# Chained block loads on GpSimd's queue, accumulating transfers by halves, and query/key pairs fetched onto both partition halves, in a gated-linear and differential attention layer

## The chip, the cores and the metric

The kernel runs on one core of a Trainium2 chip. The metric is device time in microseconds. Before the change three runs gave a median of 1126.08 us (1125.40 to 1127.34). Lower is better.

## The reference

One layer with two token mixers in parallel, for 256 tokens of width 2048, all in float32:

```python
h = rmsnorm(x, pre_norm_g)
proj = h @ w_in                      # 2048 columns in, eleven groups out
(a_q, a_k, a_v, a_g, a_lr, b_q, b_k, b_v, b_g, m_a, m_b) = split(proj)
gk  = log_sigmoid(a_lr @ gla_gk_w2 + gla_gk_b) / 16       # forget gate, rank 16
o_a = gla_chunked(a_q, a_k, a_v, gk)                      # 4 heads, 256 keys and 512 values each
lam = exp(lq1 . lk1) - exp(lq2 . lk2) + 0.2               # from diff_lambda
o_b = diff_attention(b_q, b_k, b_v, lam)                  # 16 heads: softmax(q1 k1) - lam * softmax(q2 k2)
o_a = rmsnorm(o_a, gla_norm_g) * silu(a_g);  y_a = o_a @ w_branch_a
o_b = rmsnorm(o_b, diff_norm_g) * (1 - 0.2) * silu(b_g);  y_b = o_b @ w_branch_b
out = (sigmoid(m_a) * y_a + sigmoid(m_b) * y_b) @ w_out
out = x + rmsnorm(out, post_norm_g)
```

The groups that `proj` is split into are what the kernel's keys stand for. Almost all of the time goes into products of the 256 token rows with weights that come from HBM.

## The kernel before, in words

**Weights and splits.** The weights are streamed in tiles of 128 partitions and worked on in halves of 128x1024. The products are done in the format float32r, so each half `r` is split in two: ScalarE copies it rounded to `hi` (L250), VectorE computes `lo = r - hi` (L251). TensorE then does three products for each piece, hi by the operand's hi and lo parts and lo by its hi part. `emit_half` loads and splits the next half in the list `seq`; `take` hands a half to TensorE's code after it has seen to it that the splits are AHEAD = 4 halves ahead. `hi` and `lo` have three buffers each. The scheduler fixes each engine's order of instructions before the run. GpSimd's and SyncE's queues of transfer issues are in order: an issue that waits holds all issues behind it.

**Stages.** First come the value columns `v0`, `v2`, `v3` (tasks such as the normalisation run beside). Then comes the stage that most of the change touches: six *sets*, each a 2x2 block product that is computed by seven block products rather than eight. In `phase_steps` each set runs the products in the order 1, 3, 5, 6, 2, 7, 4, each over two row blocks `t` and two halves `h`, 28 steps a set and 168 in all. A step has six matmuls. Between the steps stand 64 halves of *other* work, spread evenly: `v4`, the keys and queries of the gated attention (`k`, `q`), those of the first head group of the differential attention (`dq`, `dk`, spilled to HBM for later), and the merge gate `m00`. An other half has 12 to 16 matmuls.

**The chain of blocks.** A set's weights need sums of blocks. Four 1 MB buffers (`chain`) hold blocks a0, a1, b0, b1. `link` loads a plain block (L174, on SyncE's queue). When both halves of a block have been split for product 1 (or after an addition on VectorE, L205, for products 5 and 6), `accumulate` adds another block of HBM into the same buffer with an accumulating transfer of the whole 1 MB, issued on GpSimd's queue (L197). The blocks named c (L189) are plain loads on SyncE. A link of the next set can go when the buffer that it takes has been split for the last time.

**Banks.** Products 1, 6, 7 and 4 gather in one bank, `x`. After product 6 and again after product 7 VectorE reads that bank into `gr` (L744 after product 7), and only then may TensorE go on to add product 4. `right_done` and `left_done` put the gates on ScalarE (L700, L703, L708, L710), and `spill` (L126) writes `gr` and `gl` to HBM on GpSimd's queue; `fetch` (L131) reads back, on the same queue.

**After the sets.** `forget_gate` transposes the rank-16 columns, clears a tile and loads `w2` into four row groups (L502, L504 on GpSimd), splits it (L509, L510), and does the gate's matmuls (L519). Then follow `gla_scores`, the `ag` gates, and `diff_heads` for four groups of heads: keys and queries are computed channel by channel, scaled (L636 to L639) and spilled for each pair of heads. `diff_pair` runs as a task beside the large products: it fetches `dq` and `dk` of a pair (two transfers of 256 KB), `diff_split` makes `q2`, `kh` and `kl` (L917 to L922: six copies on ScalarE, four subtractions on VectorE, two memsets on GpSimd, each on 64 partitions), and TensorE does the scores (L952, L953), then transposes (L974), ScalarE copies them to `wt` (L976), and TensorE multiplies with the values (L982 to L984). In `q2` the hi part of a query lies on its own partition half and the lo part on the other; `kh` holds the hi part of the key on both halves, `kl` the lo part on its own half and zeros on the other. The output products end the kernel.

Of the kernel before, what the change touches and what calls it, by code (L numbers as in the profile page):

```python
# [7 lines left out]
F32R = mybir.dt.float32r  # L8
# [19 lines left out]
PRODUCTS = (1, 3, 5, 6, 2, 7, 4)  # L28
SETS = 6
LEAD = 6  # L30
EARLY = (0,)
STORED = (0, 1, 2, 3)
BIG = 18
MORE = 13
BRIDGE = 512
# [41 lines left out]
def phase_steps():  # L77

    keys = ["v4"] + [f"{name}{hf}{c}" for hf in range(2) for name in ("k", "q") for c in range(4)]
    keys += [f"{name}{g}{c}" for g in EARLY for pair in range(2) for name in ("dq", "dk") for c in (2 * pair, 2 * pair + 1)]  # L80
    keys += ["m00"]
    other = [(key, r, h) for key in keys for r in range(4 if key in ("v4", "m00") else 1) for h in range(2)]
    steps = [("set", s, prod, t, h) for s in range(SETS) for prod in PRODUCTS for t in range(2) for h in range(2)]
    mixed = []
    for i, step in enumerate(steps):
        mixed.append(step)
        mixed += other[len(other) * i // len(steps) : len(other) * (i + 1) // len(steps)]
    return mixed


# [1 line left out]
def hybrid_kernel(ctx: ExitStack, tc, xt, xn, preg, postg, w, w2, gkb, glag, lamv, diffg, ident_d, causal_d, lmask_d, out):  # L92
# [45 lines left out]
    def f32(ap):  # L138
        return ap.bitcast(F32)
# [27 lines left out]
    def weights(key, r):  # L167
        a, size = at[key][r]
        return w[a : a + P * size].rearrange("(p n) -> p n", p=P), size

    def link(s, name, t):
        count[0] += 1
        c = blocks.tile([P, 2048], F32, tag="chain", name=f"{name}_{count[0]}", bufs=4)
        sp.dma_start(c, weights(f"set{s}", {"a": 0, "b": 6}[name] + t)[0])  # L174
        chain[s, name, t] = c

    def emit_set(s, prod, t, h):
        c = slice(1024 * h, 1024 * h + 1024)
        if h == 0 and prod == 1:
            if s == 0:  # L180
                link(s, "a", t)
            link(s, "b", t)
        if h == 0 and prod == 4 and s + 1 < SETS:
            link(s + 1, "a", t)
        n = 4 * PRODUCTS.index(prod) + 2 * t + h + LEAD - 4 * PRODUCTS.index(2)
        if 0 <= n < 4:
            i, j = n // 2, n % 2
            raws[s, i, j] = u([P, 1024], "c")
            sp.dma_start(raws[s, i, j], weights(f"set{s}", 4 + i)[0][:, 1024 * j : 1024 * j + 1024])  # L189
        a, b = chain[s, "a", t], chain[s, "b", t]  # L190
        return raws[s, t, h] if prod == 2 else (b if prod in (3, 7) else a)[:, c]

    def follow_set(s, prod, t, h):
        c = slice(1024 * h, 1024 * h + 1024)

        def accumulate(name, i):
            pool.dma_start(chain[s, name, i], weights(f"set{s}", 2 + i)[0], accum_op=ALU.add)  # L197

        if prod == 1 and h == 1:
            accumulate("a", t)  # L200
        i = {(5, 1): 0, (6, 0): 1, (2, 1): 0, (7, 0): 1}.get((prod, t))
        if i is not None:
            a = chain[s, "a", i][:, c]
            second = prod in (5, 6)
            dve.tensor_tensor(out=a, in0=a, in1=chain[s, "b", i][:, c] if second else raws[s, i, h], op=ALU.add)  # L205
            if second and h == 1:
                accumulate("b", i)

    def emit_plain(j, key, r, h):
        src, size = weights(key, r)  # L210
        if h == 0:
            count[0] += 1
            raws[key, r] = wpool.tile([P, 2048], F32, tag="raw", name=f"raw_{count[0]}")
        raw = raws[key, r]
        n = size // 2
        early = key == "v0"
        if h == 0:
            if j == 0:
                load_x(0, 1)
            cuts = (0, n // 2, n, size) if j == 0 else (0, n, size) if j == 2 else (0, size)  # L220
            for a, b in zip(cuts, cuts[1:]):
# [268 lines left out]
    def forget_gate():  # L490
# [11 lines left out]
        pool.memset(w2_raw, 0.0)  # L502
        for i in range(4):
            pool.dma_start(w2_raw[32 * i : 32 * i + RANK, :], w2)  # L504
# [119 lines left out]


    gspill = [None] * (2 * SETS)
    ts, heads, m0 = {}, {}, []

    def merge_gate(banks):
# [11 lines left out]
    def others():  # L641
# [24 lines left out]
        for g in EARLY:  # L666
            for pair in range(2):
                for name in ("dq", "dk"):
                    t = t2([P, 2, S], name)
                    for c in range(2):  # L670
                        o = ps("bg")
                        for h in range(2):
                            half_channel(o, h, *take(f"{name}{g}{2 * pair + c}"))
                            if h:
                                head_part(t[:, c, :], o[:, :S], o[:, S:], name == "dk")
                                if c:
                                    heads[g, pair, name] = spill(t, name)
# [230 lines left out]

    obh, obl = [], []

    parts = {}

    def diff_split(g, pair, tq, tk):
        q2, kh, kl = parts[g, pair] = [u([P, 2, 2, S], name, F32R) for name in ("q2", "kh", "kl")]
        for m in range(2):
            own, other = slice(64 * m, 64 * m + 64), slice(64 - 64 * m, P - 64 * m)
            act.activation(q2[own, m], tq[own], AF.Copy)  # L917
            dve.tensor_tensor(out=q2[other, m], in0=tq[own], in1=f32(q2[own, m]), op=ALU.subtract)
            act.activation(kh[own, m], tk[own], AF.Copy)
            act.activation(kh[other, m], tk[own], AF.Copy)  # L920
            dve.tensor_tensor(out=kl[own, m], in0=tk[own], in1=f32(kh[own, m]), op=ALU.subtract)
            pool.memset(f32(kl[other, m]), 0.0)  # L922
        done.add(f"split{g}{pair}")
        yield

    def diff_pair(g, pair, values):
        oh, ol = obh[g], obl[g]
# [6 lines left out]
        if g in STORED:  # L934
            tq, tk = (fetch(heads[g, pair, name], name, lambda shape, name, dtype: t2(shape, name)) for name in ("dq", "dk"))
            yield
            yield from diff_split(g, pair, tq, tk)
        while f"split{g}{pair}" not in done:
            yield
        q2, kh, kl = parts[g, pair]  # L940
        vv, uu = values
        for h in (2 * pair, 2 * pair + 1):
            i2 = h % 2
# [62 lines left out]
    def diff_heads(g):  # L1006
        values = []
        if g + 2 >= SETS:
            banks = token_major(f"dv{g}", 512, x_ops, 2)
            late_u = u2 if g > 1 else u  # L1010
            vv = late_u([P, 2, 512], "dv")
            for b in range(2):
                act.activation(vv[:, b, :], banks[b], AF.Copy, scale=rstd[:, b : b + 1])
            banks = token_major(f"bg{g}", 512, x_ops, 2)
            uu = late_u([P, 2, 512], "ub")
            for b in range(2):
                gate(banks[b], b, uu[:, b, :])
            values += vv, uu
        obh.append(u2([P, 4, S], "obh", F32R))
        obl.append(u2([P, 4, S], "obl", F32R))  # L1020
        for pair in range(2):
            made = []
            for name in () if g in EARLY else ("dq", "dk"):
                t = t2([P, 2, S], name)
                for c in range(2):
                    head_part(t[:, c, :], *channel_major(f"{name}{g}{2 * pair + c}"), name == "dk")
                    pump(2)
                if g in STORED:
                    heads[g, pair, name] = spill(t, name)
                else:  # L1030
                    made.append(t)
            if made:
                tasks.insert(0, diff_split(g, pair, *made))
            tasks.append(diff_pair(g, pair, values))


# [197 lines left out]
```

## Time and profile before

| | |
|---|---|
| median of 3 runs | 1126.08 us |
| the profiled execution's own time | 1125.56 us |
| its span, first to last instruction | 1123.8 us |
| TensorE busy | 1101.0 us (98%) |
| VectorE, ScalarE, GpSimd busy | 852.1, 688.2, 105.6 us |
| mean granted TensorE clock | 0.996 |
| moved by the DMA engines | 264.06 MB |

The page gives the busy time of each engine, then the span in 40 equal slices with the busy share of each in tenths, then the DMA queues, the chain of work that ended last, the costliest groups of instructions, and the DMA issues with their median time to landing. A row of the timeline reads: start, duration, engine, line, operation, the tile written and the tiles read, shape and count, and in brackets the engine's idle time before it and what ended that.

### The profile page before, as it was taken

The page shows a single profiled execution, that of the slowest core. Times are in us where ns is not written, and L with a number is a line of the kernel's source. Part 1 is how long each engine was busy: PE and PEld are TensorE (multiplying, and loading weights), DVE is VectorE, ACT ScalarE, POOL GpSimd, SP SyncE. Part 2 cuts the span into 40 slices and gives each one's busy share as a digit, 9 for nine tenths or more (in the row PEclk, how much of TensorE's full clock was granted, in tenths as well). Part 3 has the DMA queues.
Part 4 walks back from the last instruction along what each step waited for, and adds up shares of the span by engine and source line. Part 5 has one row for each costly group of instructions (what it writes and reads, how often), then busy time and mean ns, then how long its engine had stood idle before and what let it go on. Part 6 is the DMA issues. An engine that isn't in the chain of part 4 may idle for free.

```text
span 1123.8 us, 15119 instructions
## 1 busy us (share of the span) xinstructions
PE 1101.0 (98%) x5546; PEld 941.8 (84%) x5546; DVE 852.1 (76%) x1192; ACT 688.2 (61%) x1011; POOL 105.6 (9%) x173
## 2 busy tenths in 40 slices
PE   8999999999999999999999999999999999999996
PEld 7997887888888888877888888888888888888886
DVE  7877969889798897966998667786777865656463
ACT  7855666666666676669555556676767664444450
POOL 0100010010101001020000221121202020000000
PEclk9999999999999999999999999999999999999999
DMA  8797897887979879666554946575677575556752
GB/s 315 259 413 206 237 327 195 334 214 224 288 214 360 209 247 316 160 213 251 187 183 159 372 153 225 179 249 210 206 245 251 200 278 197 188 187 215 272 187 76
DMA packets 47834, 264.06 MB, mean 235 GB/s; under 512 B 6096, under 2 KB 7632, under 8 KB 25232
## 3 DMA queue, kind: packets, MB, share of 16 engines
q1 hardware_dynamic: 31968, 196.50, 48.9%
q0 software_dynamic: 14784, 65.28, 21.0%
q10 hardware_dynamic: 1008, 1.32, 0.4%
q8 instruction: 43, 0.70, 0.3%
q14 instruction: 31, 0.25, 0.1%
HBM read 241.06 MB, written 22.02 MB: 234 GB/s over the span
## 4 chain that ended last, share of the span: by engine, by line
PE 85%; issue 5%; DMA 4%; ACT 2%; DVE 2%; POOL 0%; DVEq 0%; SPq 0%; POOLq 0%; ACTq 0%
PE mm L437 38%; PE mm L726 15%; PE bg L459 6%; PE mm L459 6%; DMA a<-in_w_dram 3%; PE bg L461 3%; PE mm L461 3%; PE bg L437 2%; PE bg L420 2%; PE mm L405 2%; PE mm L420 2%; DVE lo L251 1%; ACT hi L250 1%; PE bg L829 1%; PE bg L405 1%
## 5 line engine op out<-in xcount | busy, mean ns | idle before, releaser
L251 DVE TENSOR_TENSOR lo<-raw,hi 128x1024 fp32r<-128x1024 f32 (+3 forms) x291 | 345.3, 1188 | 153.9 <-ACT hi L250 144.7
L250 ACT ACTIVATE hi<-raw 128x1024 fp32r<-128x1024 f32 (+3 forms) x291 | 298.9, 1030 | 230.7 <-PE mm L437 140.1
L437 PE MATMUL mm<-hi,xs 128*128 128x512 f32 (+1 forms) x576 | 139.7, 384 | 0.0
L250 ACT ACTIVATE hi<-a 128x1024 fp32r<-128x1024 f32 x96 | 101.2, 1059 | 62.0 <-PE bg L459 19.8
L251 DVE TENSOR_TENSOR lo<-a,hi 128x1024 fp32r<-128x1024 f32 x96 | 116.4, 1220 | 26.2 <-ACT hi L250 24.8
L437 PEld LDWEIGHTS mm<-hi,xs 128*128 128x128 f32 x576 | 106.4, 188 | 16.4
L459 PE MATMUL mm<-xs,hi 128*128 128x512 f32 x384 | 101.3, 396 | 0.0
L459 PE MATMUL bg<-xs,hi 128*128 128x512 f32 x384 | 99.5, 390 | 0.7 <-ACT hi L250 0.7
L459 PEld LDWEIGHTS bg<-xs,hi 128*128 128x128 f32 x384 | 72.1, 188 | 15.3 <-ACT hi L250 1.1
L726 PE MATMUL mm<-hi,xs 128*128 128x512 f32 x288 | 77.9, 392 | 2.6 <-DVE gr L744 2.6
L459 PEld LDWEIGHTS mm<-xs,hi 128*128 128x128 f32 x384 | 69.2, 189 | 11.6
L437 PE MATMUL mm<-lo,xs 128*128 128x512 f32 (+1 forms) x288 | 74.5, 380 | 0.0
L251 DVE TENSOR_TENSOR lo<-b,hi 128x1024 fp32r<-128x1024 f32 x48 | 58.3, 1219 | 12.6 <-ACT hi L250 11.8
L250 ACT ACTIVATE hi<-b 128x1024 fp32r<-128x1024 f32 x48 | 50.7, 1060 | 24.1 <-PE bg L459 10.8
L726 PEld LDWEIGHTS mm<-hi,xs 128*128 128x128 f32 x288 | 53.1, 188 | 13.2 <-issue 2.3
L437 PEld LDWEIGHTS mm<-lo,xs 128*128 128x128 f32 x288 | 54.0, 188 | 9.0
L461 PEld LDWEIGHTS bg<-xs,lo 128*128 128x128 f32 x384 | 52.4, 190 | 4.1 <-DVE lo L251 0.3
L461 PEld LDWEIGHTS mm<-xs,lo 128*128 128x128 f32 x384 | 52.4, 190 | 3.8
L963 ACT ACTIVATE prob<-prob,mx,score_scale 128x128 f32<-128x128 f32 x64 | 34.3, 537 | 31.9 <-DVE mx L958 31.9
L461 PE MATMUL bg<-xs,lo 128*128 128x256 f32 x384 | 53.8, 282 | 0.0
L461 PE MATMUL mm<-xs,lo 128*128 128x256 f32 x384 | 53.5, 282 | 0.0
L437 PE MATMUL mm<-hi,oah 128*128 128x512 f32 x128 | 50.9, 397 | 0.0
(299 smaller groups left out, 2074.5 us busy)
## 6 DMA issues: line engine op xcount, KB each, us to landing
raw<-in_w_dram SPq DMA_DIRECT2D x128, 1024.0 KB, 5.1
a<-in_w_dram SPq DMA_DIRECT2D x12, 1024.0 KB, 6.9
b<-in_w_dram SPq DMA_DIRECT2D x12, 1024.0 KB, 8.0
c<-in_w_dram SPq DMA_DIRECT2D x24, 512.0 KB, 11.4
a<-in_w_dram POOLq DMA_DIRECT2D x12, 1024.0 KB, 14.1
b<-in_w_dram POOLq DMA_DIRECT2D x12, 1024.0 KB, 10.6
raw<-in_w_dram SPq DMA_DIRECT2D x14, 832.0 KB, 6.1
dq<-dq POOLq DMA_DIRECT2D x16, 256.0 KB, 3.7
```

The source lines that it names most:

```text
L250: act.activation(hi_t[:, a:b], r[:, a:b], AF.Copy)
L251: dve.tensor_tensor(out=lo_t[:, a:b], in0=r[:, a:b], in1=f32(hi_t[:, a:b]), op=ALU.subtract)
L405: i = pe.matmul(out, lhs, rhs, start=first and n == 0, stop=last and n == len(pairs) - 1)
L420: i = pe.matmul(banks[g][b][:, :n], a[part][:, P * b : P * b + P], w[:, n * g : n * g + n], start=first, stop=last)
L437: i = pe.matmul(banks[b][:, :n], a[part][:, P * b : P * b + P], w[:, n * j : n * j + n], start=first, stop=last)
L459: i = pe.matmul(o, hi[:, c], x_pair(kt), start=kt == 0, stop=kt == KT - 1)
L461: i = pe.matmul(o[:, :S], lo[:, c], x_ops(kt)[0], start=False, stop=False)
L726: i = pe.matmul(out, a[part], w[:, 512 * j : 512 * j + 512], start=first, stop=last, skip_group_check=out is x)
L829: pe.matmul(o, xk[:, P * c : P * c + P], xq.rearrange("p (b c t) -> p b c t", b=2, c=4)[:, :, c, :], start=i == 0, stop=i == 1)
L963: act.activation(prob[m][:, lo:up], prob[m][:, lo:up], AF.Exp, scale=score_scale[:, b : b + 1], bias=mx[:, i : i + 1], accum_out=z[:, i : ...
```

## The change

- **Order of the set stage.** FRONT = 4 other halves come one after each of the first four steps; the remaining 60 are spread over the 168 steps.
- **Block loads.** Set 0's a0 and a1 are linked when the first half of `v3` is emitted, its b0 and b1 at product 1, on SyncE as before. For sets 1 to 5 all four links are issued on GpSimd's queue, at earlier steps of the emission: a0 at (product 7, t = 1), a1 at (4, 0), b0 at (4, 1), b1 at (1, 0) of the set itself.
- **Accumulating transfers by halves.** Each 128x1024 half goes out behind its own split (or addition): 48 transfers of 512 KB for 24 of 1 MB.
- **Forget gate.** `w2_raw` is allocated before the set stage; its memset and four loads go ahead of `m00`, and the task loses its first step.
- **Pairs of the differential attention.** `diff_split` is gone. `twice` fetches the pair's `dq` into a raw tile and its `dk` into `kl`, each onto both partition halves: four transfers of 256 KB a pair. ScalarE then makes `q2` and `kh` with one full-width copy each, VectorE subtracts twice for `q2` on 64x512 and once for the whole `kl`. There are no memsets, and `kl` holds the lo part on both halves. `STORED` goes; all groups are spilled and fetched, as they were.

```diff
     mixed, put = [], 0
     for i, step in enumerate(steps):
         mixed.append(step)
-        mixed += other[len(other) * i // len(steps) : len(other) * (i + 1) // len(steps)]
+        due = min(i + 1, FRONT) + (len(other) - FRONT) * (i + 1) // len(steps)
+        mixed += other[put:due]
+        put = due
...
-        sp.dma_start(c, weights(f"set{s}", {"a": 0, "b": 6}[name] + t)[0])
+        (pool if s else sp).dma_start(c, weights(f"set{s}", {"a": 0, "b": 6}[name] + t)[0])
...
-        if h == 0 and prod == 1:
-            if s == 0:
-                link(s, "a", t)
-            link(s, "b", t)
-        if h == 0 and prod == 4 and s + 1 < SETS:
-            link(s + 1, "a", t)
+        if h == 0 and s + 1 < SETS and (prod, t) in ((7, 1), (4, 0)):
+            link(s + 1, "a", 1 - t)
+        if h == 0 and s + 1 < SETS and (prod, t) == (4, 1):
+            link(s + 1, "b", 0)
+        if h == 0 and prod == 1 and (s == 0 or t == 0):
+            link(s, "b", t if s == 0 else 1)
...
-            pool.dma_start(chain[s, name, i], weights(f"set{s}", 2 + i)[0], accum_op=ALU.add)
-
-        if prod == 1 and h == 1:
+            pool.dma_start(chain[s, name, i][:, c], weights(f"set{s}", 2 + i)[0][:, c], accum_op=ALU.add)
+
+        if prod == 1:
             accumulate("a", t)
...
-            if second and h == 1:
+            if second:
                 accumulate("b", i)
...
+        if key == "v3" and r == 0 and h == 0:
+            for i in range(2):
+                link(0, "a", i)
...
-        w2_raw, w2_s = u([P, 1024], "w2_raw"), u([P, 1024], "w2_s", F32R)
-        pool.memset(w2_raw, 0.0)
-        for i in range(4):
-            pool.dma_start(w2_raw[32 * i : 32 * i + RANK, :], w2)
-        yield
+        w2_s = u([P, 1024], "w2_s", F32R)
...
+        pool.memset(w2_raw, 0.0)
+        for i in range(4):
+            pool.dma_start(w2_raw[32 * i : 32 * i + RANK, :], w2)
         banks = [ps("bg"), ps("bg")]
         for q in range(KT // 2):
             half_tile(banks, 512, q, x_ops, *take("m00"))
...
-    def diff_split(g, pair, tq, tk):
...
+    def twice(t, d):
+
+        for h in range(2):
+            rows = slice(64 * h, 64 * h + 64)
+            pool.dma_start(f32(t[rows]), d.rearrange("(m p) i t -> p m i t", m=2))
...
-            tq, tk = (fetch(heads[g, pair, name], name, lambda shape, name, dtype: t2(shape, name)) for name in ("dq", "dk"))
-            yield
-            yield from diff_split(g, pair, tq, tk)
...
+        raw = u([P, 2, 2, S], "dq")
+        q2, kh, kl = (u([P, 2, 2, S], name, F32R) for name in ("q2", "kh", "kl"))
+        twice(raw, heads[g, pair, "dq"])
+        twice(kl, heads[g, pair, "dk"])
+        yield
+        act.activation(q2, raw, AF.Copy)
+        act.activation(kh, f32(kl), AF.Copy)
+        for m in range(2):
+            other = slice(64 - 64 * m, P - 64 * m)
+            dve.tensor_tensor(out=q2[other, m], in0=raw[other, m], in1=f32(q2[other, m]), op=ALU.subtract)
+        dve.tensor_tensor(out=kl, in0=f32(kl), in1=f32(kh), op=ALU.subtract)
+        yield
```

More of the change, by code (lines that the diff above doesn't have):

```diff
@@ L30 @@
 LEAD = 6
+FRONT = 4
 EARLY = (0,)
-STORED = (0, 1, 2, 3)
 BIG = 18
@@ L83, in phase_steps @@
     steps = [("set", s, prod, t, h) for s in range(SETS) for prod in PRODUCTS for t in range(2) for h in range(2)]
-    mixed = []
+    mixed, put = [], 0
     for i, step in enumerate(steps):
         mixed.append(step)
-        mixed += other[len(other) * i // len(steps) : len(other) * (i + 1) // len(steps)]
+        due = min(i + 1, FRONT) + (len(other) - FRONT) * (i + 1) // len(steps)
+        mixed += other[put:due]
+        put = due
     return mixed
@@ L626, in hybrid_kernel @@
     gspill = [None] * (2 * SETS)
+    w2_raw = u([P, 1024], "w2_raw")
     ts, heads, m0 = {}, {}, []
@@ L909, in hybrid_kernel @@
     obh, obl = [], []
-    parts = {}
-    def diff_split(g, pair, tq, tk):
[L914 to L923, printed above, removed]
-        yield
+    def twice(t, d):
+        for h in range(2):
+            rows = slice(64 * h, 64 * h + 64)
+            pool.dma_start(f32(t[rows]), d.rearrange("(m p) i t -> p m i t", m=2))
     def diff_pair(g, pair, values):
@@ L933, in diff_pair @@
             values.extend(fetch(gspill[2 * g + 4 + i], name, u) for i, name in enumerate(("dv", "ub")))
-        if g in STORED:
-            tq, tk = (fetch(heads[g, pair, name], name, lambda shape, name, dtype: t2(shape, name)) for name in ("dq", "dk"))
-            yield
-            yield from diff_split(g, pair, tq, tk)
-        while f"split{g}{pair}" not in done:
-            yield
-        q2, kh, kl = parts[g, pair]
+        raw = u([P, 2, 2, S], "dq")
[10 more added lines that the diff above has]
+        yield
         vv, uu = values
@@ L1021, in diff_heads @@
         for pair in range(2):
-            made = []
             for name in () if g in EARLY else ("dq", "dk"):
@@ L1027, in diff_heads @@
                     pump(2)
[L1028 to L1033, printed above, removed]
+                heads[g, pair, name] = spill(t, name)
             tasks.append(diff_pair(g, pair, values))
```

## The prediction

> **What bounds the kernel now.** I read the page first: busy time, the slices, and the chain that ended last.
>
> ```profile
> span 1123.8 us, 15119 instructions
> PE 1101.0 (98%) x5546; PEld 941.8 (84%) x5546; DVE 852.1 (76%) x1192; ACT 688.2 (61%) x1011; POOL 105.6 (9%) x173
> ...
> PEclk9999999999999999999999999999999999999999
> DMA  8797897887979879666554946575677575556752
> ...
> PE 85%; issue 5%; DMA 4%; ACT 2%; DVE 2%; POOL 0%; DVEq 0%; SPq 0%; POOLq 0%; ACTq 0%
> ```
>
> TensorE is the bound: busy for 1101.0 of 1123.8 us. The change gives it the same products, so it can win back only idle time (1123.8 − 1101.0 = 22.8 us, ends included) and time at a lower clock; anything that makes TensorE late costs in full. The table of windows says where that idle time lies (columns: window, length, busy time and count of PE, PEld, DVE, ACT and POOL, then granted clock, DMA share, GB/s).
>
> ```profile
> 75.00:100.00 25.00, 25.00 (x124) 22.64 (x123) 17.84 (x19) 14.95 (x18) 2.87 (x4) 1.00 1.03 329
> 100.00:125.00 25.00, 22.94 (x101) 19.64 (x100) 21.70 (x21) 16.16 (x18) 1.73 (x2) 0.93 0.68 172
> 125.00:150.00 25.00, 22.85 (x113) 19.62 (x112) 20.07 (x21) 16.69 (x21) 1.65 (x3) 1.00 0.81 286
> 175.00:200.00 25.00, 24.20 (x119) 19.98 (x119) 24.96 (x27) 15.73 (x18) 1.41 (x2) 1.00 0.68 156
> ```
>
> TensorE's timeline names the gaps ahead of the kernel's end, which the change does not touch (the last bracket: us idle, and what ended it).
>
> ```profile
> 103.23 0.50 PE L726 MATMUL mm<-hi,r1h 128*128 128x512 f32 x1 [2.00 <-ACT hi L250]
> 140.47 1.15 PE L726 MATMUL mm<-hi,xs 128*128 128x512 f32 x4 [2.15 <-DVE gr L744]
> 278.42 2.11 PE L459 MATMUL bg<-xs,hi 128*128 128x512 f32 x8 [0.71 <-ACT hi L250]
> 347.92 0.93 PE L726 MATMUL mm<-hi,xs 128*128 128x512 f32 x3 [0.40 <-DVE gr L744]
> 483.88 0.50 PE L437 MATMUL bg<-hi,xs 128*128 128x512 f32 x1 [0.69 <-ACT hi L250]
> 511.11 1.07 PE L519 MATMUL bg<-lrt,w_s 128*128 128x256 f32 x7 [1.30 <-issue]
> 695.74 0.30 PE L953 MATMUL bg<-kl,q 128*128 128x128 f32 x1 [0.72 <-DVE kl L921]
> 709.54 0.49 PE L982 MATMUL bg<-dv,wt 128*128 128x128 f32 x2 [1.46 <-ACT wt L976]
> ```
>
> These eight make 9.43 us; with 0.80 in 175 to 200 and the clock's loss in 100 to 125 that is what any part of the change can reach.
>
> **Step 1: set 0's accumulating transfers (FRONT, halves, early links).** The rows are the issue on GpSimd's queue, the same transfer in the chain, the split that needed it, and one "other" half on TensorE with the set half behind it.
>
> ```profile
> 86.01 0.88 POOL L197 DMA_DIRECT2D a<-in_w_dram  x1 [0.84 <-DVE vl L551]
> ...
> 86.01 16.01 DMA a<-in_w_dram
> ...
> 102.13 1.06 ACT L250 ACTIVATE hi<-a 128x1024 fp32r<-128x1024 f32 x1 [5.19 <-DMA a<-in_w_dram]
> ...
> 112.89 1.61 PE L437 MATMUL bg<-hi,xs 128*128 128x400 f32 x8
> 115.06 0.40 PE L726 MATMUL mm<-hi,s2h 128*128 128x512 f32 x1
> ...
> 141.91 1.07 PE L726 MATMUL mm<-hi,xs 128*128 128x512 f32 x4
> 143.27 1.07 PE L726 MATMUL mm<-hi,xs 128*128 128x512 f32 x4
> ```
>
> The transfer takes 16.01 us, ACT waits 5.19 for it, and TensorE, four halves behind, idles 2.00. Behind that gap the granted clock is 0.93 over 25 us, a loss of 0.07 × 25 = 1.75 us. The change moves this read later against the issue: the second block's first half goes out one set half earlier (143.27 − 141.91 = 1.36 us), and three more "other" halves lie in between (115.06 − 112.89 = 2.17 us each): 1.36 + 3 × 2.17 = 7.9 us, more than the 5.19 by which ACT was late, before counting that half a block should land sooner than a whole one. So the wait goes: −(2.00 + 1.75) = −3.75, call it −3.7. Bounds: −3.75 if all goes, 0 if the transfers stretch by as much. I take the full end because 7.9 exceeds 5.19.
>
> The Trainium skill, page "TensorE: Matmul & The Clock Gate", section "HAM oscillation — how this bites in real kernels", says that only TensorE gaps above about 3.4 us bring the clock down. By that rule the 2.00 gap has no clock loss to give back, and this term would be −2.0 and the sum 1.7 us smaller. The trace shows 0.93 behind a gap of 2.00 and 1.00 around the longer gap of 2.15, so length alone does not decide here; the measurement stands.
>
> **Step 2: set 1's second block.** ACT waits for an accumulated block once more:
>
> ```profile
> 172.75 2.01 ACT L250 ACTIVATE hi<-a 128x1024 fp32r<-128x1024 f32 x2 [3.53 <-DMA a<-in_w_dram]
> ```
>
> TensorE loses 0.80 in that window. Here the first half gains the 1.36 us of one set half, and half of the bytes to wait for; the lateness is 3.53. The page's medians to landing bound what the bytes are worth:
>
> ```profile
> a<-in_w_dram SPq DMA_DIRECT2D x12, 1024.0 KB, 6.9
> ...
> a<-in_w_dram POOLq DMA_DIRECT2D x12, 1024.0 KB, 14.1
> ```
>
> If a half takes half of 14.1, 7 us come off; if nothing, 1.36. I take −0.8 (bounds −0.8 and 0), since 3.53 − 1.36 = 2.17 is under a third of 7.
>
> **Step 3: the handover between product 7 and product 4.** DVE must read the bank (gr, L744) before TensorE writes on in it. FRONT leaves ten "other" halves to each set in one fixed pattern, where before it drifted.
>
> ```profile
> 139.64 0.68 DVE L744 TENSOR_TENSOR gr<-mm,p 128x512 f32<-128x512 f32 x1
> ...
> L726 PE MATMUL mm<-hi,xs 128*128 128x512 f32 x288 | 77.9, 392 | 2.6 <-DVE gr L744 2.6
> ```
>
> The group's 2.6 is 2.15 + 0.40 of the list above; with 0.71 and 0.69 (sets 2 and 5, an "other" half between, its split late) six handovers cost 3.95. In the changed program's order five of the six stand like sets 2 and 5, and after set 2 product 4 follows directly and must wait for the 0.68 us add and about 0.2 around it: 5 × 0.71 + 0.9 = 4.45, so +0.5. Bounds: none visible, as in sets 1 and 4 (−3.95), and 2.15 in all six (12.9 − 3.95 = +8.95).
>
> **Step 4: forget gate's w2 early.** The memset and four loads that stood after the merge gate (L502, L504) go ahead of it.
>
> ```profile
> 494.39 0.97 POOL L502 MEMSET w_raw<- 128x1024 f32 x1
> 497.22 1.94 POOL L504 DMA_DIRECT2D w_raw<-in_w_dram  x4
> 508.64 1.06 ACT L509 ACTIVATE w2h<-w_raw 64x1024 fp32r<-64x1024 f32 x1 [0.68 <-DMA w_raw<-in_w_dram]
> ```
>
> At 508.64 ACT waits for the load; the L519 matmuls then idle TensorE 1.30 at 511.11. With the data there for tens of us, their place in the program follows ready operands: −1.3 (bounds −1.3 and 0). On Pool the 0.97 + 1.94 now stand among set 5's block links; at worst those issue 2.9 us later, hidden while their data is needed later than that.
>
> **Step 5: diff attention.** Per pair, two fetches become four (256 KB each), ten split instructions and two memsets become five and none.
>
> ```profile
> 682.52 0.55 POOL L126 DMA_DIRECT2D dk<-dk  x1 [15.07 <-DVE dk L639]
> 683.06 0.54 POOL L131 DMA_DIRECT2D dq<-dq  x1
> ...
> 688.70 1.29 ACT L917 ACTIVATE q<-dq 64x512 fp32r<-64x512 f32 x2 [3.13 <-DMA dq<-dq]
> ...
> 694.90 0.69 DVE L921 TENSOR_TENSOR kl<-dk,kh 64x512 fp32r<-64x512 f32 x1
> ```
>
> One pair's fetch (683.06) stood behind a spill that waited 15.07 us for DVE; ACT then waited 3.13, kl came at 694.90, and TensorE lost 0.72 on kl and 1.46 on the wt behind it. In the changed order both fetches stand ahead of that spill: −2.2. A full-width kl subtraction (1.2 us, an estimate from the 0.69 of half the width) now sits in front of TensorE's scores where two of 0.69 stood; I book 0.4 for it: −1.8 (bounds −2.2, and +1.4 if the two gaps stay and one more of 1.4 joins). The other pairs show no gap; ACT falls from 6 × 0.65 to 2 × 1.06 us a pair.
>
> **Step 6: twenty block loads on GpSimd's queue.**
>
> ```profile
> 129.80 0.33 SPq L174 DMA_DIRECT2D a<-in_w_dram  x1
> 143.08 1.06 ACT L250 ACTIVATE hi<-a 128x1024 fp32r<-128x1024 f32 x1 [0.30 <-PE mm L726]
> 150.76 0.53 POOL L126 DMA_DIRECT2D gl<-gl  x1 [8.85 <-ACT gl L708]
> 151.37 0.89 POOL L197 DMA_DIRECT2D a<-in_w_dram  x1
> ```
>
> The links can't really go sooner: they wait for buffers freed by the same splits as before. On Pool each issue costs 0.89: 20 × 0.89 = 17.8 us, and 24 more accumulate issues at 0.53 to 0.89 are 13 to 21, and the 16 more fetches of step 5 (0.54) 9, beside 105.6 busy; Pool bounds nothing. What is queued behind a waiting link: the gr spill, the next accumulates, the gl spill. The a accumulates now stand ahead of gl's 8.85 wait, in part. I book 0 (bounds −0.5 and the price of rival C), covered by the spare time of a link: the one issued at 129.80 lands after some 6.9, near 136.7, and its first split starts at 143.08, so 6.4 us later.
>
> Fewer "other" halves in sets 1 to 5 (10 for 10.7) put more set halves against DVE, which is busy 24.96 of 25 in 175 to 200: +0.3, an estimate (0.7 × 5 halves, a tenth of a us each).
>
> **Sum**: −3.7 − 0.8 + 0.5 − 1.3 − 1.8 + 0.3 = −6.8, against the profiled execution's own 1125.56 (span 1123.8, 1.76 around it): 1118.8. The median shown, 1126.08, is 0.5 above it: 1119.3.
>
> **Rivals.** 0.2% is 2.25 us, about what a measurement of this kernel tells from none.
>
> B: the accumulates stay late because the DMA engines are full, not because they start late. For: 1.03 DMA share in 75 to 100, just while they run; early links add load there. Against: the same bytes as before, 7.9 us more room. Then steps 1 and 2 give nothing; steps 3 to 5 leave −2.3: 1123.8, on the bound.
>
> C, slower: links and accumulates share one queue. Before, block loads ran beside the accumulates from SP; now a 1 MB load of 7 to 14 us stands ahead of the next set's accumulates in Pool's queue. It decides once accumulates land some 3 us later: 3.53 us of lateness cost TensorE 0.80 and 5.19 cost 2.00 and a clock dip, 3.75. A slip of 5 us on both a blocks in each of the sets 1 to 5 costs 5 × 2.0 or so at the bare gap, 10 to 11: 1130; with the dip each time 5 × 3.75 = 18.8: 1138. For: DMA share of 0.68 to 1.03 in the set windows. Against: halves need half of the bytes, and links issue well ahead of the accumulates. The Trainium skill, page "DMA: Bandwidth & Descriptors", sections "Queues, rings and completion order" and "SWDGE vs HWDGE vs iDMA", supports this rival: each DMA engine takes turns between queue rows, while one ring drains in its order, and a plain load belongs on the hardware path. No run before shows a plain block load on Pool's queue.
>
> D: the new pattern makes the handover 2.15 in all six sets, as in set 0: +8.95 in place of +0.5, so 1127.8. For: 2.15 is the worst that the trace shows. Against: sets 2 and 5, with the order that five sets now have, paid 0.7.
>
> E: handovers vanish as in sets 1 and 4 too: −4.5 more, about 1114.8.
>
> **How the numbers follow.** Forecast (A) 0.50; B 0.14 (faster 0.08, same 0.06); C 0.18, slower; D 0.10 (same 0.05, slower 0.04, faster 0.01); E 0.08. Faster 0.50 + 0.08 + 0.01 + 0.08 = 0.67; same 0.06 + 0.05 = 0.11; slower 0.18 + 0.04 = 0.22. The time is A's, with 1116.5 to 1122.5 of its own. The range runs from 1114.0 (below E) to 1130.0 (C's cheaper half), which leaves out the rest of C, some 0.1, and little beside.
>
> **What would show it.** Step 1: no ACT wait of some us on an accumulated block near 100 us, clock 1.00 there. Step 2: PE 25.00 between set 1's products. Step 3: gaps of 0.7, not 2, ended by hi or gr. Step 4: no gap at the w2 matmuls. Step 5: no gap ended by kl or wt. Step 6: links on Pool landing in 7 to 14 us, no ACT wait on them. The prediction is wrong if ACT waits on a or b in sets 1 to 5, if "gr" ends gaps of 2 us, or if q2 or kl ends new ones.

## The result and the profile after

The changed kernel takes 1138.47 us (median of 4 runs, 1134.93 to 1141.18) against 1125.96 (1125.40 to 1127.34): a ratio of 1.0107 with a 95% interval of 1.0073 to 1.0142. It is slower by about 12.5 us. The profiled execution, 1141.18 us with a span of 1139.4, is the longest of the four.

The page of the changed kernel, the lines that answer to those of before:

```profile
span 1139.4 us, 15115 instructions
PE 1107.3 (97%) x5546; PEld 942.7 (83%) x5546; DVE 848.3 (74%) x1184; ACT 675.0 (59%) x979; POOL 142.0 (12%) x217
...
PEclk9999999999999999999999999989999999999998
DMA  9899797796988879676555965756858675556751
...
PE 84%; DMA 6%; issue 3%; DVE 3%; ACT 2%; POOL 1%; DVEq 0%; SPq 0%; POOLq 0%; ACTq 0%
```

TensorE is still the bound, ScalarE and VectorE have less to do, and yet idle time (1139.4 − 1107.3 = 32.1 us, 9.3 more) and time at a lower clock have both grown. TensorE is busy 6.3 us longer for the same 5546 matmuls; by the windows below the clock took 5.25 us (0.07 × 25 + 0.14 × 25), 3.5 more than before, and the other 2.8 are not accounted for here. The windows say where (columns as before; first three windows of the kernel before, then those of the changed one):

```profile
300.00:325.00 25.00, 25.00 (x127) 21.28 (x126) 22.83 (x22) 15.57 (x18) 1.71 (x2) 1.00 0.98 289
650.00:675.00 25.00, 25.00 (x145) 21.88 (x145) 17.32 (x29) 15.94 (x30) 4.82 (x8) 1.00 0.46 159
725.00:750.00 25.00, 25.00 (x130) 21.16 (x129) 21.00 (x39) 22.61 (x43) 7.00 (x12) 1.00 0.66 230
```

```profile
75.00:100.00 25.00, 25.00 (x129) 23.42 (x128) 15.57 (x18) 14.92 (x19) 4.65 (x6) 1.00 1.00 286
100.00:125.00 25.00, 25.00 (x122) 21.83 (x121) 23.94 (x24) 17.47 (x19) 4.54 (x6) 1.00 0.99 277
175.00:200.00 25.00, 25.00 (x125) 21.17 (x124) 24.99 (x25) 16.61 (x19) 3.42 (x4) 1.00 0.77 190
225.00:250.00 25.00, 23.15 (x113) 18.96 (x112) 17.30 (x18) 13.83 (x16) 2.77 (x5) 1.00 0.98 280
300.00:325.00 25.00, 22.77 (x110) 18.40 (x109) 17.53 (x16) 14.17 (x16) 2.18 (x3) 1.00 0.88 236
650.00:675.00 25.00, 22.58 (x129) 19.33 (x127) 18.46 (x29) 16.25 (x29) 9.46 (x14) 1.00 0.75 224
675.00:700.00 25.00, 24.89 (x140) 21.74 (x141) 16.56 (x30) 11.26 (x16) 1.14 (x2) 0.93 0.53 184
725.00:750.00 25.00, 19.82 (x102) 16.53 (x102) 17.27 (x41) 14.40 (x30) 6.43 (x8) 0.86 0.63 179
```

Set 0 (100 to 125) and set 1 (175 to 200) are now full, as predicted. New holes stand in sets 2 and 3 (225 to 250, 300 to 325) and, larger, in the differential attention (650 to 750), with the clock's loss behind two of them. TensorE's timeline names what ended the gaps:

```profile
143.44 0.50 PE L464 MATMUL bg<-xs,hi 128*128 128x512 f32 x1 [0.72 <-ACT hi L255]
246.96 0.50 PE L731 MATMUL mm<-hi,r1h 128*128 128x512 f32 x1 [1.79 <-ACT hi L255]
281.43 0.47 PE L731 MATMUL mm<-hi,xs 128*128 128x512 f32 x1 [0.88 <-DVE gr L749]
318.26 0.50 PE L731 MATMUL mm<-hi,r1h 128*128 128x512 f32 x1 [2.17 <-ACT hi L255]
420.25 0.50 PE L464 MATMUL bg<-xs,hi 128*128 128x512 f32 x1 [0.94 <-ACT hi L255]
506.67 0.48 PE L520 MATMUL bg<-lrt,w_s 128*128 128x256 f32 x2 [0.38 <-issue]
674.96 0.55 PE L894 MATMUL bg<-ident,ua 128*128 128x128 f32 x3 [2.42 <-DVE ua L887]
742.68 0.48 PE L975 MATMUL bg<-ident,prob 128*128 128x128 f32 x1 [4.99 <-DVE prob L971]
```

Both traces have 4866 matmuls with split weights. Counted through the timelines, the changed kernel is 2.6 us behind at the 2593rd (after the sets) and 15.5 behind at the 4105th (in the output products), and stays so. In this execution, then, 2.6 us were lost up to the end of the set stage, where the prediction had won some 5, and 12.9 in the differential attention, where it had won 1.8.

The list of waits has ScalarE's, which are new in the attention (us in total, times, longest):

```profile
ACT hi L255 <- DMA a<-in_w_dram: 15.7, 4, 5.9
...
ACT q L935 <- DMA dq<-dq: 15.2, 6, 4.3
...
ACT kh L936 <- DMA kl<-dk: 9.3, 5, 4.2
```

Before, ScalarE waited 3.13 us for dq in one place and 0.72 for dk in another; now 24.5 us for dq and dk. The largest gap, step by step in the changed kernel's timeline:

```profile
732.20 2.21 POOL L346 TENSOR_TENSOR de<-de,neg_half 128x2 f32<-128x2 f32 x1 [4.80 <-DVE de L992]
734.37 0.62 POOL L920 DMA_DIRECT2D dq<-dq  x1
...
738.60 1.06 ACT L935 ACTIVATE q<-dq 128x1024 fp32r<-128x1024 f32 x1 [3.60 <-DMA dq<-dq]
...
742.27 0.75 DVE L971 SCALAR_TENSOR_TENSOR prob<-prob,c,prob 128x128 f32<-128x128 f32 x2
```

The second half of a pair's dq stands on GpSimd's queue behind a 128x2 operation that waits for VectorE; ScalarE waits for that transfer; the exponentials of another pair are queued behind its q; prob comes at 742.27, and TensorE, whose order is fixed too, stood still for 4.99 us.

### The profile page after: what moved, and what is told of

Same layout as the page of the kernel before. It is cut to its first block, busy times and chain, and to the rows that moved or that the text cites. A ratio compares the mean times of both kernels' runs of the same rounds, so it can differ in the third digit from the quotient of the medians.

```text
span 1139.4 us, 15115 instructions
## 1 busy us (share of the span) xinstructions
PE 1107.3 (97%) x5546; PEld 942.7 (83%) x5546; DVE 848.3 (74%) x1184; ACT 675.0 (59%) x979; POOL 142.0 (12%) x217
## 4 chain that ended last, share of the span: by engine, by line
PE 84%; DMA 6%; issue 3%; DVE 3%; ACT 2%; POOL 1%; DVEq 0%; SPq 0%; POOLq 0%; ACTq 0%
PE mm L442 37%; PE mm L731 17%; PE bg L464 7%; PE mm L464 5%; PE bg L466 3%; DMA a<-in_w_dram 3%; PE bg L442 3%; PE mm L466 3%; DMA dq<-dq 2%; DVE lo L256 2%; PE bg L425 2%; PE mm L410 2%; PE mm L425 2%; ACT hi L255 1%; PE bg L834 1%
## 5 line engine op out<-in xcount | busy, mean ns | idle before, releaser
L442 PE MATMUL mm<-hi,obh 128*128 128x512 f32 x128 | 50.5, 394 | 0.0
```

The source lines that it names most:

```text
L442: i = pe.matmul(banks[b][:, :n], a[part][:, P * b : P * b + P], w[:, n * j : n * j + n], start=first, stop=last)
```

## The experiments

All times are medians; "before" is the kernel before on the same chip, measured anew in each round; intervals are of the ratio. Only the single transfer is more than 2% from before; the others are told from it, or not, by their intervals. Where two rows have different values of before, a difference of their times is one across rounds; the values of before differ by up to 1.2 us.

| kernel | us | before | ratio (95%) |
|---|---|---|---|
| step 5 alone | 1137.08 | 1125.41 | 1.0096 (1.0078 to 1.0115) |
| all but step 5 | 1127.86 | 1125.41 | 1.0020 (1.0008 to 1.0032) |
| all but step 5, links on SyncE | 1134.63 | 1125.41 | 1.0077 (1.0057 to 1.0097) |
| all but step 5, whole accumulates | 1132.46 | 1125.41 | 1.0058 (1.0037 to 1.0078) |
| pairs fetched into the large pool | 1127.56 | 1126.61 | 1.0016 (1.0006 to 1.0026) |
| whole change, splits two steps later | 1132.66 | 1126.61 | 1.0051 (1.0030 to 1.0072) |
| all but step 5, c on GpSimd | 1122.38 | 1126.61 | 0.9964 (0.9953 to 0.9975) |
| FRONT alone | 1138.87 | 1126.61 | 1.0110 (1.0092 to 1.0127) |
| FRONT alone, later pattern | 1128.03 | 1126.01 | 1.0026 (1.0015 to 1.0037) |
| all but step 5, c on GpSimd, later pattern | 1118.16 | 1126.01 | 0.9933 (0.9914 to 0.9952) |
| step 5 alone, one transfer each | 1229.51 | 1126.01 | 1.0917 (1.0893 to 1.0941) |
| before, four issues a pair | 1125.41 | 1126.01 | 0.9997 (0.9985 to 1.0009) |
| large pool, four issues of 128 KB | 1127.23 | 1125.40 | 1.0018 (1.0007 to 1.0028) |
| large pool, four issues of 256 KB | 1133.31 | 1125.40 | 1.0073 (1.0053 to 1.0093) |

### Which part costs: step 5 alone, and all but step 5

The first adds the diff's last part (`twice` and the full-width splits, for `diff_split`) to the kernel before; the second takes that part out of the changed kernel and leaves the rest.

```diff
-            yield from diff_split(g, pair, tq, tk)
+        twice(raw, heads[g, pair, "dq"])
+        twice(kl, heads[g, pair, "dk"])
+        yield
+        act.activation(q2, raw, AF.Copy)
...
```

> The kernel before with step 5 alone: pairs fetched onto both halves, split by full-width instructions. Theory 1 (the pair's splits stand in ScalarE's fixed order ahead of other work and wait for fetches that GpSimd's queue issues late): +10 to +14 us over before, with ScalarE idle 15 us or more ahead of q and kh for dq and dk, and gaps of 2 us or more on TensorE ended by ua or prob. Rival (the loss comes only in the surroundings that the other parts make; the step itself does what was predicted): -2 to 0 us.

> The changed kernel with the pairs of the differential attention as before, all other parts kept. Theory 1: what is left of the loss is that of the set stage, +2 to +4 us over before, and the gaps ended by ua and prob are gone. Rival (the loss behind the sets comes from another part, for instance the memory that early w2 holds): +10 us or more. The prediction's own steps 1 to 4 without step 5 would give -5.

Step 5 alone costs 11.7 us, all the rest 2.4; together 14.1, near the whole loss of 12.5. With step 5 alone ScalarE's waits on dq and kl are 9.0 + 13.0 us, and the gaps ended by ua and prob are back (2.30 and 4.64 us).

```profile
ACT kh L931 <- DMA kl<-dk: 13.0, 6, 4.4
...
ACT q L930 <- DMA dq<-dq: 9.0, 4, 3.7
```

Counted by matmuls as above, step 5 alone is level with before at the 2593rd (0.0 us) and 11.3 behind at the 4105th: its whole cost arises in the differential attention. Theory 1 holds as to the place; the step's cost does not need the other parts around it.

### The set stage: the queue of the links, and halves

```diff
-        (pool if s else sp).dma_start(c, weights(...)[0])
+        sp.dma_start(c, weights(...)[0])
```

```diff
-            pool.dma_start(chain[s, name, i][:, c], weights(...)[0][:, c], accum_op=ALU.add)
+            pool.dma_start(chain[s, name, i], weights(...)[0], accum_op=ALU.add)      # behind the second half
```

> As the changed kernel without step 5, but the twenty block loads go on SyncE's queue at the same steps. Theory 2 (block loads and accumulates share one queue, and b1's load holds back the accumulates of its own set; rival C of the prediction): the accumulates of a land about 4 us sooner in sets 2 and 3, the two gaps of 1.9 and 2.3 us ended by an accumulated a go, so 3 to 5 us faster than the changed kernel without step 5. Rival (the wait comes from the bytes on the DMA engines, whatever the queue): within 1 us of it.

> As the changed kernel without step 5, but each accumulating transfer is of a whole 1 MB block again, behind both halves. If halves help (prediction, steps 1 and 2): slower than the changed kernel without step 5 by 2 to 6 us, with longer waits of ScalarE for a. Rival (the half that lands last sets the wait, and it lands when the whole block would): within 1 us.

Theory 2 fell: with the links on SyncE the kernel is not faster but 6.8 us slower than with them on GpSimd. SyncE's timeline around set 1, first with links on GpSimd, then with links on SyncE, shows one thing that moved:

```profile
140.37 0.33 SPq L228 DMA_DIRECT2D raw<-in_w_dram  x1
141.22 1.18 SPq L192 DMA_DIRECT2D c<-in_w_dram  x2
```

```profile
150.06 0.33 SPq L177 DMA_DIRECT2D b<-in_w_dram  x1
150.49 1.65 SPq L192 DMA_DIRECT2D c<-in_w_dram  x3
```

A link waits for its buffer, and on SyncE's queue it holds the c loads behind it: three of them go at 150.49, just ahead of set 1's accumulates (issued from 152.60 on), where without the links the last two went at 141.22. The last half of a then lands 19.2 us after its issue (14.9 with the links on GpSimd), and ScalarE waits for accumulated blocks six times, 16.9 us in all, in place of four times and 11.5. The holding up is read from this one stretch; c on GpSimd's queue with the links on SyncE was not tried.

Without halves the kernel is 4.6 us slower, as predicted. The longer waits of ScalarE that were expected with it did not show: 7.7 us in three places with whole blocks, 11.5 in four with halves. The two profiled executions differ by only 1.6 us, so where the 4.6 us arise stays open.

### Set 3: the c loads

In the changed kernel the four c loads of set 3 (SyncE) go out with the accumulates of a (GpSimd), and the chain shows the last of these:

```profile
289.36 3.53 SPq L191 DMA_DIRECT2D c<-in_w_dram  x4
```

```profile
290.79 0.89 POOL L199 DMA_DIRECT2D a<-in_w_dram  x1 [2.86 <-DVE lo L256]
...
297.98 0.86 POOL L199 DMA_DIRECT2D a<-in_w_dram  x1 [1.18 <-DVE lo L256]
```

```profile
297.98 19.06 DMA a<-in_w_dram
```

```diff
-            sp.dma_start(raws[s, i, j], weights(f"set{s}", 4 + i)[0][...])
+            pool.dma_start(raws[s, i, j], weights(f"set{s}", 4 + i)[0][...])
```

> As the changed kernel without step 5, but the c loads go on GpSimd's queue too, so that in sets 2 and 3 they stand behind the accumulates of a. Theory 4 (in set 3 the four c loads of 512 KB, issued with the accumulates, take the DMA engines from them, and the last half of a lands after 19.9 us): the gap of 3.1 us near 318 and the clock's dip behind it go, 4 to 6 us faster than the changed kernel without step 5, near 1122 to 1124. Rival (order within GpSimd's queue holds the accumulates): no faster, and more gaps on c.

It is 5.5 us faster than all but step 5 (ratios to before of 0.9964 and 1.0020) and faster than the kernel before. The windows of sets 2 and 3 in this kernel:

```profile
225.00:250.00 25.00, 25.00 (x126) 21.29 (x126) 20.90 (x21) 15.69 (x18) 6.05 (x10) 1.00 1.04 286
300.00:325.00 25.00, 25.00 (x127) 21.28 (x126) 22.49 (x22) 15.92 (x18) 3.48 (x4) 1.00 1.01 287
```

In the same windows TensorE of all but step 5 was busy 24.93 and 22.03 us, so most of the gain lies in set 3; its gap there was 2.97 us, with the clock at 0.86 over that window. The DMA engines are no emptier than before (1.04, 1.01), but the c bytes now come behind the accumulates, in one queue, and TensorE is not held up. The last half of a lands 14.97 us after its issue, in place of 19.06 (19.87 in all but step 5), and the last c lands at 314.35, near the 314.42 of the changed kernel. The Trainium skill, "DMA: Bandwidth & Descriptors", section "Queues, rings and completion order", says that each DMA engine takes turns between queue rows and drains a ring in its order. The runs fit that: on another queue 2 MB of c shared the engines with the accumulates and the last half took 19.06 us, on the same queue it took 14.97. They do not prove it, since the order of the issues changed as well: the first c goes out at 294.89, just behind the last accumulate (294.34), where it went out at 289.36, ahead of the first. A later start of c on SyncE's own queue was not tried.

### FRONT, alone and with its other halves laid later

Only `phase_steps` is changed, first as in the change, then with 84 added to the quotient that places the 60 halves:

```diff
-        due = min(i + 1, FRONT) + (len(other) - FRONT) * (i + 1) // len(steps)
+        due = min(i + 1, FRONT) + ((len(other) - FRONT) * (i + 1) + 84) // len(steps)
```

> The kernel before with the four front halves alone (the order of the set stage), nothing else. Prediction, step 1: without halves the room is 3 x 2.17 + 1.36 - 1.36 = 6.5 us, still over the 5.19, so set 0's gap and the clock's dip go: -3.7, the handovers +0.5 to +1, so -3 us. Rival (other waits take the place): between -1 and +2 us, with accumulated blocks late in later sets, which have fewer other halves to cover them.

> The kernel before with the four front halves alone, but the other 60 halves laid 84/168 of a step pattern later, so that in sets 1 to 5 three of them, not two, stand between the split of a block for product 1 and its reading for product 5. Theory 5 (FRONT alone costs 12 us because each later set lost an other half in just that stretch, 2.2 to 2.8 us of cover for the accumulate): 6 to 14 us faster than the front halves alone, 1125 to 1132 us. Rival (the cost is that sets 1 to 5 have ten other halves, wherever these stand): within 2 us of the front halves alone, 1139.

FRONT alone missed both expectations: 12.3 us slower. Set 0's wait is gone, but the later sets wait (list of waits, before and with FRONT alone, and TensorE's timeline with FRONT alone in sets 1 and 4):

```profile
ACT hi L250 <- DMA a<-in_w_dram: 13.6, 4, 5.2
```

```profile
ACT hi L253 <- DMA a<-in_w_dram: 27.6, 7, 5.1
```

```profile
181.03 0.50 PE L729 MATMUL mm<-hi,r1h 128*128 128x512 f32 x1 [2.15 <-ACT hi L253]
...
393.25 0.50 PE L729 MATMUL mm<-hi,r1h 128*128 128x512 f32 x1 [1.64 <-ACT hi L253]
```

The order written by `phase_steps` gives the reason. In sets 1 to 5 of the kernel before, two or three other halves stand between the set's second step, which sends out a0's accumulate, and the ninth, which reads it, and two or three between the fourth and the eleventh (a1), five or six together; with FRONT there are two and two in each. Moving the pattern makes them three and three, with the same ten halves a set, and 10.8 of the 12.3 us come back (across rounds; 11.9 us of waits on a are left, in three places). Where the halves stand decides, not their number.

> The changed kernel without step 5, with the c loads on GpSimd's queue and the other halves in that later pattern. Theory 5: ScalarE's waits on an accumulated a, still 6 us in all with the c loads moved, go to near zero, 0 to 2 us faster than the c loads alone (1122.4). Rival (the window is wide enough already): the same within 1 us.

With both, the waits on an accumulated a are gone from the list, and the kernel takes 1118.16 us: 0.9933 of before, the fastest here. It gained more than was expected (4.2 us over the c loads alone, across rounds).

### Step 5: place, count, bytes, form

In the kernel before, a pair's fetch waits for a buffer of the small pool; in the changed one its target is in the large pool, and the order lets fetch and splits go earlier, among the gssq work. The first edit here changes that target alone, the second moves the changed kernel's splits two steps of the task back; TensorE's order in the attention changes with it.

```diff
-  lambda shape, name, dtype: t2(shape, name)
+  lambda shape, name, dtype: u([P, 2, 2, S], name)[:, 0]
```

```diff
         twice(kl, heads[g, pair, "dk"])
         yield
+        yield
+        yield
         act.activation(q2, raw, AF.Copy)
```

> The kernel before, only that a pair's dq and dk are fetched into tiles of the large pool (u) in place of the small one (t2); two transfers of 256 KB and ten split instructions a pair as before. In its order of instructions the first pairs' fetches and splits now stand among the gssq work, as in the changed kernel. Theory 3 (where the splits stand is what costs, and they stand there because their buffers are free earlier): +6 to +12 us over before, with waits of ScalarE on dq and dk of 10 us or more. Rival (the four longer transfers and the full-width instructions cost): within 2 us of before.

> The changed kernel whole, with two more steps of the pair's task between its fetches and its splits. Theory 3 (ScalarE waits for transfers that the order puts just ahead): the waits of ScalarE on dq and kl fall from 24 us to under 10 us, and 4 to 10 us of the 12.9 behind the sets come back: 1129 to 1135 us. Rival (the transfers and the instructions themselves cost): within 2 us of the changed kernel.

The early place alone costs 1 to 2 us, so theory 3 as put fell; but with the splits later the whole change gains 5.8 us, and one wait on dq is left (2.5 us):

```profile
ACT q L937 <- DMA dq<-dq: 2.5, 1, 2.5
```

So the place costs more where the transfers take long. The waits are not the whole of the step's cost: with them all but gone the kernel is still 4.8 us slower than all but step 5 (1132.66 against 1127.86, across rounds). Two further edits: one transfer of 512 KB for each of dq and dk, with the instructions in the order of step 5 alone; and, on the kernel before, four issues of 128 KB.

```diff
-        for h in range(2):
-            pool.dma_start(f32(t[64 * h : 64 * h + 64]), d.rearrange("(m p) i t -> p m i t", m=2))
+        src = d.rearrange("p m n -> p (m n)")      # spilled as 64 rows of 1024
+        pool.dma_start(f32(t).rearrange("p m i t -> p (m i t)"), bass.AP(src.tensor, src.offset, [[0, 2]] + [list(x) for x in src.ap]))
```

```diff
-        pool.dma_start(t, d)
+        for r in (slice(0, 64), slice(64, P)):
+            pool.dma_start(t[r], d[r])
```

> The kernel before with step 5 alone, but each of a pair's dq and dk comes by one transfer of 512 KB onto both halves in place of two of 256 KB (the spill writes the pair's rows so that one read can serve both); the order of the other instructions is that of step 5 alone. Theory 6 (GpSimd's queue holds the second transfers behind the gssq and de work, which waits for VectorE, and ScalarE waits for them): 5 to 10 us faster than step 5 alone (1137), ScalarE's waits on dq and kl from 22 us to under 12. Rival (bytes: 1 MB a pair takes that long to land): within 2 us of 1137.

> The kernel before, with dq and dk of a pair each fetched by two transfers of 64 partitions (128 KB) in place of one of 256 KB, all else as before: four issues a pair, the same bytes, splits in their old places. Theory 6 as a matter of the count of issues alone: +4 us or more over before. Rival (four issues cost only where the splits stand right behind them): within 1.5 us of before.

Four issues cost nothing by themselves. The single transfer told nothing about issues, since it is a far slower transfer (the page's DMA issues: KB each, median us to landing):

```profile
dq<-dq POOLq DMA_DIRECT2D x8, 512.0 KB, 18.5
kl<-dk POOLq DMA_DIRECT2D x8, 512.0 KB, 17.2
```

The spill that goes with it, which writes the pair as 64 rows, is slower too: 12.3 us for dq at the median, against 5.0 in step 5 alone.

The last two keep the early place, the ten splits and four issues, in one order of instructions, and differ in what an issue moves: 128 KB onto 64 partitions, both read, or 256 KB onto 128 partitions, of which the first is read by nobody.

```diff
-        t = u([P, 2, 2, S], name)[:, 0]
-        for r in (slice(0, 64), slice(64, P)):
-            pool.dma_start(t[r], d[r])
-        return t
+        t = u([P, 2, 2, S], name)
+        for i in (1, 0):
+            pool.dma_start(t[:, i], d)
+        return t[:, 0]
```

> As the fetch into the large pool, but each of dq and dk comes by two transfers of 64 partitions (128 KB): four issues a pair, the bytes of before, splits in the early places among the gssq work. Theory 7 (what is left of step 5's cost is the bytes, a pair's last transfer landing 10 to 12 us behind its first issue where half the bytes took 7 to 8): +1 to +4 us over before, as with two issues. Rival (the issues, of which two stand behind waiting gssq and de work): +8 us or more.

> The same order and the same four issues a pair, but each issue moves a whole 256 KB and the first of the two is one that nobody reads, so a pair moves 1 MB as in step 5; ten split instructions as before. Theory 7 (bytes): +6 us or more over before, with ScalarE's waits on dq and dk over 10 us. Rival (neither: the full-width splits, which need all of a pair's transfers at once, cost): within 2 us of the four small transfers.

1127.23 against 1133.31: with the bytes doubled the early place costs 6.1 us more. How much of that is the bytes is less sure: in the two profiled executions, 6.7 us apart, 2.3 lie ahead of the 2593rd matmul, where the programs are the same, and 4.5 in the differential attention. Nor do ScalarE's waits on dq and dk explain it: they came to 2.5 + 4.2 us, under the 10 expected and little above the 1.0 + 3.1 of the small transfers. That the larger transfers cost is shown; by which wait is not. From 1133.31 to step 5 alone, 3.8 us more: the two differ in the full-width splits, which need both halves at once, and in that dk goes straight into kl. Which of these it is was not tried. Counted within the attention of the profiled executions alone, early place, bytes and the rest come to 2.1, 4.5 and 4.6 us, in place of 1.8, 6.1 and 3.8 by the medians.

## Why the prediction was wrong

- **Step 1, right.** Set 0's wait and the clock's loss behind it (3.75 us) are gone: 25.00 busy at 1.00 from 75 to 125. That the gap cost any clock hung on where it fell (last section).
- **Step 2, right in its place and wrong beyond it.** Set 1 shows 25.00 from 175 to 200. But the same wait came up in sets 2 and 3 (1.79 and 2.17 us of TensorE), which the step did not look at.
- **Step 3, right.** Six handovers of 0.72, 0.72, 0.88, 0.72, 0.94 and 0.70 make 4.68, for 4.45 predicted.
- **Step 4, right, mis-sized.** The gap at the w2 matmuls went from 1.30 to 0.38: −0.9, not −1.3.
- **Step 5, the step that failed.** It was booked at −1.8 with a bound of +1.4; alone it costs 11.7. The prediction saw that fetches move ahead of the blocking spill. It counted the 16 more issues as Pool's time, and the extra 4 MB (512 KB for each of eight pairs) not at all. It did not count that the splits move forward with the fetches in ScalarE's fixed order (the second pair's first split from 688.70 to 663.3), right behind transfers of twice the bytes, with the gla and softmax work queued behind. ScalarE's waits on dq and dk went from 3.85 to 24.5 us. By the medians the cost is 1.8 for the early place, 6.1 for the bytes and 3.8 for the rest (2.1, 4.5 and 4.6 within the attention); what makes up the rest stays open.
- **Step 6, wrong in sign.** Booked at 0 and seen as a danger (rival C), the links on GpSimd's queue are worth 6.8 us in this order; set 1's timeline puts it down to SyncE's c loads, which the links no longer hold up. The result, 1138.47, comes out at the upper end of C's span of 1130 to 1138 by chance: on balance the shared queue helped, and 11.7 us of the loss came from another step.
- **The +0.3 for fewer other halves, the second failure.** In the unit of the sum this term is what FRONT takes from later sets: alone it makes the kernel 12.3 us slower while saving set 0's 3.75. The prediction priced it by VectorE's load, not by the cover that the accumulates lose. Halves (4.6) and links on GpSimd (6.8), both measured in all but step 5, come to 11.4 us, for the 9.9 that this kernel, at +2.4, has back of the 12.3.

## What to carry to other kernels

When a load is moved forward in a program of fixed orders, look at who reads it and how far behind it now stands: an in-order engine that reaches the reader early passes the wait on to everything queued behind. Filler work that covers a latency should be counted in the very stretch that it covers, for each repetition, not as a total. Among transfers that compete, issuing the less urgent one behind the urgent one in the same queue can be worth more than a queue of its own (5.5 us here).

## What was not expected of the hardware

A transfer whose source repeats 64 rows onto two halves of 128 partitions (512 KB) took 18.5 us (dq) and 17.2 (dk) to land at the median, where two of 256 KB on 64 partitions took 5.3 and 6.8 each in step 5 alone; why was not looked into.

And the clock: behind gaps of 2.00 (before), 2.15 (FRONT alone, set 1), 2.42 and 4.99 us the windows of 25 us show 0.93, 0.93, 0.93 and 0.86, but 1.00 behind 2.15 (before) and 2.17 us. The Trainium skill, "TensorE: Matmul & The Clock Gate", section "HAM oscillation — how this bites in real kernels", puts the bound near 3.4 us; the 0.93 behind gaps of 2.00 to 2.42 does not fit that. Shorter windows of the traces show what decides. The clock falls to 0.50 for 3.41 us at a time (or two or more times that), and within a run these stretches begin on a fixed grid with a step of 3.41 us. Here are four windows of that grid in the kernel before, the first two at the gap of 2.00, the others at that of 2.15:

```profile
101.33:104.74 3.41, 1.44 (x5) 0.92 (x6) 1.53 (x2) 2.61 (x3) 0.00 (x0) 1.00 0.00 0
104.74:108.15 3.41, 3.41 (x11) 3.18 (x11) 3.41 (x4) 1.10 (x2) 0.87 (x1) 0.50 0.34 38
135.46:138.87 3.41, 2.86 (x17) 2.34 (x15) 3.24 (x5) 1.82 (x2) 0.55 (x1) 1.00 0.93 333
138.87:142.28 3.41, 1.81 (x8) 1.56 (x9) 1.45 (x2) 1.28 (x2) 0.53 (x1) 1.00 1.06 419
```

The gap of 2.00 leaves 1.97 us idle in one window, and the next runs at 0.50; that of 2.15 is cut by a border into 0.55 and 1.60, and nothing happens (the changed kernel's 2.17 into 1.54 and 0.69). In all 16 traces, the first 8 and the last 12 us left out, the 23 windows at full clock with 1.74 us idle or more, about half, were each followed by 0.50, and none with 1.72 or less was. So a gap of 2 us costs 1.7 us of clock or nothing, by where it falls.
